# A mixture of 32 experts on one core: SwiGLU once an expert, weighted one-hots on ScalarE, float32 matmuls in larger groups, first-layer weights by 2 MB

## The chip, the cores and the metric

The kernel is one program on one core of a Trainium2 chip. The metric is the device time of one execution in microseconds; lower is better. The engines named below are TensorE (PE, its weight loads PEld), VectorE (DVE), ScalarE (ACT), GpSimd (POOL) and SyncE (SP), which here only issues transfers.

## The reference

Two model blocks over 256 tokens of width 1024, in float32. The first has two layers of feed-forward network, mixer and feed-forward network; the second has a mixer and then the part that the change touches, a mixture of 32 experts of which each token takes 4:

```python
logits = tokens @ w_router + b_router
top_logits, top_idx = lax.top_k(logits, 4); top_w = softmax(top_logits)
# for each expert e, for the tokens that chose it:
hid = tokens[rows] @ w_exp_in[e] + b_exp_in[e]            # 1024 -> 2048
x_glu = minimum(hid[..., ::2], 7);  x_lin = clip(hid[..., 1::2], -7, 7)
out = (x_glu * sigmoid(1.702 * x_glu) * (x_lin + 1)) @ w_exp_out[e] + b_exp_out[e]   # 1024 -> 1024
y[rows] += out * top_w
```

After it come a gate, the addition to x and a last rmsnorm.

## The kernel before, in words

All weights are float32 in HBM, 713 MB with the rest, and pass through the core once, in the order of use, as a **stream** (class `Stream`) of chunks of 128 rows x 2048 columns, 1 MB. SyncE issues a chunk's load (L272) as soon as its **place** is free. A chunk is split by halves (`convert`): ScalarE writes `wh`, the half rounded to the matmul's short float32 format (L284), and VectorE writes `wl`, the remainder `raw - wh` (L285). TensorE multiplies with both. There are five pairs `wh`, `wl`, so the conversions run up to five halves ahead of TensorE. `get()` hands out the next pair; each call is one **step**, and `later(PRE or POST, n, f)` puts off a piece of work by n steps, ahead of or behind the conversions of that step. All queues follow the order in which the program issues, which this code lays down by hand.

In the dense part, up to some 1600 us, the stream has three places of 1 MB (pool `raw`). At the end of the second mixer four buffers of 1 MB that are no longer needed (`p2`, tags r0 to r3) become places too, and the two of `xt` once each; in the experts' part the seven places take the chunks in turn.

The experts' part is the function `moe`. Each expert has 64 slots, and one-hot matrices gather the tokens into them (`Group`, four experts at a time; `gather`). A loop runs q = 0 to 132; q = 4 e + j calls `hidden(e, j)`, which multiplies the slots with a quarter of the first-layer weights (two chunks `exp_in`, four steps), and from q = 5 on `outputs`, a quarter of the second layer of the expert before (one chunk `exp_out`, two steps). `folded` brings a quarter of the hidden units, copied out of PSUM as `hs`, into the transposed form by float32 matmuls `pf`, and after every second quarter runs the SwiGLU on half an expert's units: add the bias (L1555), clip (L1556, L1557), multiply (L1558), sigmoid on ScalarE (L1562), multiply (L1563), and split into two parts `act` (L1564 on ScalarE, L1565 on VectorE). When both quarters of an output half are summed, `combine` adds it to the tokens' sums `y` by float32 matmuls (L1523) with weighted, transposed one-hots `ohw`. These come from `wdup`, one-hot times weight, made on GpSimd (L1493) and turned by TensorE (L1500). A float32 matmul stands as two records in the trace.

```python
        for q in range(4 * NE + 5):
            e, j = divmod(q, 4)
...
                hidden(e, j)
            if q >= 5:
                outputs(*divmod(OUT_ORDER[q - 5], 4))
```

## Time and profile before

| | us |
|---|---|
| median of three runs (lowest, highest) | 2688.63 (2688.14, 2689.32) |
| the profiled execution, its span | 2688.0 |
| TensorE, VectorE, ScalarE busy in it | 2605.0, 2080.7, 1723.2 |
| the experts' stretch shown below, 1700 to 2600 us: VectorE busy | 890.54 of 900 |

The profile records one execution; busy times are sums over its instructions, and a share over the whole span mixes the dense part, to some 1600 us, with the experts' part after it. Tables by stretches keep them apart. A matmul's end is modelled, so that a busy TensorE is not TensorE at its peak.

### The profile page before, as it was taken

To read this page: it belongs to the slowest core of one execution; us is meant where nothing else is said; L and a number is where in the kernel's file an instruction comes from. 1 tells how busy PE (TensorE), PEld (TensorE's weight loads), DVE (VectorE), ACT (ScalarE), POOL (GpSimd) and SP (SyncE) were. 2 spreads that over 40 slices of the span, in tenths; PEclk is the share of its full clock that TensorE was granted. 3 is DMA by queue.
4 is the path that set the end of the run, shared out by engine and by line. 5 is a ranking of instruction groups with operands and counts; after the bars stand their busy time and mean duration, and the time that the engine had idled before them with its cause. 6 is when DMAs were issued, how large, how long until landed. Compare 5 with 4: busy or idle time off the path is not lost.

```text
span 2688.0 us, 34842 instructions
## 1 busy us (share of the span) xinstructions
PE 2605.0 (97%) x12700; PEld 2092.6 (78%) x12700; DVE 2080.7 (77%) x2717; ACT 1723.2 (64%) x2290; POOL 182.6 (7%) x255
## 2 busy tenths in 40 slices
PE   8999999999999999999999998999999999999996
PEld 6889888887787978778798886777777777777775
DVE  5656766666666676655656679999999999999997
ACT  5444554444444454544555538989898989888886
POOL 1000000001101000000000102000000000000000
PEclk9999999999999999999999999999999999999999
DMA  7655445655566444565444566999999999999995
GB/s 282 220 216 207 153 149 192 221 218 211 213 225 245 149 153 172 193 226 180 158 149 151 175 246 251 381 399 389 381 393 388 386 388 391 388 393 389 390 395 203
DMA packets 106227, 712.89 MB, mean 265 GB/s; under 512 B 13380, under 2 KB 14052, under 8 KB 25409
## 3 DMA queue, kind: packets, MB, share of 16 engines
q1 hardware_dynamic: 92976, 667.03, 65.9%
q0 software_dynamic: 12928, 43.05, 4.3%
q8 instruction: 101, 1.65, 0.2%
q14 instruction: 78, 0.63, 0.1%
q10 hardware_dynamic: 144, 0.52, 0.0%
HBM read 709.40 MB, written 3.77 MB: 265 GB/s over the span
## 4 chain that ended last, share of the span: by engine, by line
PE 84%; DVE 9%; issue 3%; ACT 3%; DMA 0%; POOL 0%; DVEq 0%; SPq 0%; ACTq 0%; POOLq 0%
PE hid L1536 7%; PE hid L1537 6%; DVE wl L285 6%; PE po L1580 3%; PE pf L1549 3%; PE g L347 3%; PE u L347 3%; PE g L348 3%; PE u L349 3%; PE g L349 3%; PE u L348 3%; PE d L347 3%; PE d L349 3%; PE d L348 3%; PE y L1523 3%
## 5 line engine op out<-in xcount | busy, mean ns | idle before, releaser
L285 DVE TENSOR_TENSOR wl<-raw,wh 128x1024 fp32r<-128x1024 f32 (+2 forms) x1274 | 1504.7, 1218 | 424.7 <-ACT wh L284 414.9
L284 ACT ACTIVATE wh<-raw 128x1024 fp32r<-128x1024 f32 (+2 forms) x1274 | 1294.3, 1050 | 527.7 <-PE d L349 126.5
L1536 PE MATMUL hid<-wh,xgt 128*128 128x512 f32 x1024 | 441.0, 431 | 0.2 <-ACT hs L1539 0.2
L1537 PE MATMUL hid<-wl,xgt 128*128 128x512 f32 x1024 | 404.8, 395 | 0.0
L1580 PE MATMUL po<-wl,act 128*128 128x512 f32 x512 | 208.6, 407 | 32.9 <-DVE wl L285 32.9
L1536 PEld LDWEIGHTS hid<-wh,xgt 128*128 128x128 f32 x1024 | 193.3, 189 | 54.3 <-issue 16.1
L1537 PEld LDWEIGHTS hid<-wl,xgt 128*128 128x128 f32 x1024 | 193.3, 189 | 53.3 <-issue 14.3
L1579 PE MATMUL po<-wh,act 128*128 128x512 f32 x512 | 204.0, 398 | 2.8 <-ACT osb L1584 2.8
L1580 PEld LDWEIGHTS po<-wl,act 128*128 128x128 f32 x512 | 96.1, 188 | 78.5 <-DVE wl L285 57.6
L347 PE MATMUL g<-wh,xth 128*128 128x512 f32 (+1 forms) x384 | 147.0, 383 | 0.0
L347 PE MATMUL u<-wh,xth 128*128 128x512 f32 (+1 forms) x384 | 146.0, 380 | 0.0
L348 PE MATMUL g<-wl,xth 128*128 128x512 f32 (+1 forms) x384 | 144.8, 377 | 0.0
L349 PE MATMUL g<-wh,xtl 128*128 128x512 f32 (+1 forms) x384 | 144.5, 376 | 0.0
L349 PE MATMUL u<-wh,xtl 128*128 128x512 f32 (+1 forms) x384 | 144.4, 376 | 0.0
L348 PE MATMUL u<-wl,xth 128*128 128x512 f32 (+1 forms) x384 | 144.1, 375 | 0.0
L347 PE MATMUL d<-wh,hth 128*128 128x512 f32 x352 | 139.8, 397 | 0.0
L349 PE MATMUL d<-wh,htl 128*128 128x512 f32 x352 | 138.8, 394 | 0.0
L348 PE MATMUL d<-wl,hth 128*128 128x512 f32 x352 | 138.8, 394 | 0.0
L1549 PEld LDWEIGHTS pf<-fold,hs 128*128 128x128 f32 x1024 | 130.8, 192 | 8.8 <-issue 1.3
L1549 PE MATMUL pf<-fold,hs 128*128 128x64 f32 x1024 | 129.1, 269 | 1.4 <-DVE v L1555 0.9
L1523 PE MATMUL y<-osb,ohw 128*128 128x512 f32 x256 | 123.0, 603 | 2.1 <-ACT osb L1584 2.1
L1493 POOL TENSOR_TENSOR wdup<-oh,wgt 128x128 f32<-128x128 f32 x64 | 72.5, 1162 | 741.4 <-PE wts L1500 510.0
(488 smaller groups left out, 4441.6 us busy)
## 6 DMA issues: line engine op xcount, KB each, us to landing
raw<-d_exp_in SPq DMA_DIRECT2D x256, 1024.0 KB, 7.3
raw<-d_dense SPq DMA_DIRECT2D x245, 1024.0 KB, 4.8
raw<-d_exp_out SPq DMA_DIRECT2D x128, 1024.0 KB, 7.5
ada_w<-d_ada POOLq DMA_DIRECT2D x96, 256.0 KB, 4.6
bias<-tables POOLq DMA_DIRECT2D x2, 1920.0 KB, 12.7
bg<-d_b_gate POOLq DMA_DIRECT2D x12, 256.0 KB, 4.2
raw<-d_dense SPq DMA_DIRECT2D x4, 768.0 KB, 4.5
raw<-d_dense SPq DMA_DIRECT2D x5, 512.0 KB, 3.6
```

What stands on the lines that cost most here:

```text
L284: A.activation(hi[:, :w], r[:, h * w:h * w + w], AF.Copy)
L285: V.tensor_tensor(lo[:, :w], r[:, h * w:h * w + w], hi[:, :w], OP.subtract)
L347: T.matmul(ps, lhsT=xh, rhs=wh, start=start, stop=False)
L348: T.matmul(ps, lhsT=xh, rhs=wl, start=False, stop=False)
L349: T.matmul(ps, lhsT=xl, rhs=wh, start=False, stop=stop_)
L1493: G.tensor_tensor(d[:, :, c], oh, wg, OP.mult)
L1523: T.matmul(y[t][n], lhsT=grp[e // 4].w[:, e % 4, t], rhs=osb[e, n], start=e == 0, stop=e == NE - 1)
L1536: T.matmul(ph, lhsT=lhs, rhs=wh[:, 512 * i:512 * i + 512], start=k == 0, stop=False)
L1537: T.matmul(ph, lhsT=lhs, rhs=wl[:, 512 * i:512 * i + 512], start=False, stop=k == 7)
L1549: T.matmul(pf[:, 4 * (c // 2) + 2 * (j % 2) + c % 2], lhsT=hs[:, 128 * c:128 * c + 128], rhs=fold, start=True, stop=True)
L1579: T.matmul(po, lhsT=lhs, rhs=wh[:, 512 * i:512 * i + 512], start=k == 0, stop=False)
L1580: T.matmul(po, lhsT=lhs, rhs=wl[:, 512 * i:512 * i + 512], start=False, stop=k == 7)
```

## The change

It has four parts, all in the experts' part; the dense part's instructions keep their order.

1. **SwiGLU once an expert.** `folded` is called once for two quarters, does their `pf` matmuls in one group, and adds the bias into half of `v`, which now holds a whole expert. `activate` does the rest over 512 columns after the second half; the last expert still goes by halves.
2. **Weighted one-hots on ScalarE**: eight copies with a scale per group of four experts, in place of GpSimd's eight multiplications.
3. **`combine` once an expert**: the four matmuls `y` of both output halves follow one another.
4. **First-layer weights by 2 MB.** Two chunks `exp_in` become one of 128 x 4096. Places are kept by size: r0 to r3 and the dense places 0 and 1 become three places of 2 MB, `xt` one of 2 MB used once; the chunks `exp_out` keep the third dense place, and from q = 14 a second one, `hx`, in the space of the pool `bp`, which is given up at q = 14 in place of 26 (`bias_part` and `bias_sum` move to q = 8, 10 and 12 for it). The two rows that `gated_sum` and `final` need are loaded at q = 128 into a place. The two parts of a converted half lie in one tile `w`.

```diff
-        a["w_exp_in_2"][0].reshape(NE, 2, 4, 128, 4, 256, 2).transpose(0, 4, 1, 3, 2, 6, 5)
-    ).reshape(NE, 4, 2, 128, 2048)
+        a["w_exp_in_2"][0].reshape(NE, 2, 4, 128, 4, 256, 2).transpose(0, 4, 3, 1, 2, 6, 5)
+    ).reshape(NE, 4, 128, 4096)
...
+            self.todo = {w: [i for i, (_, n) in enumerate(chunks) if (n > 2048) == (w > 2048)] for w in (2048, 4096)}
+            self.own = raw.tile([128, 2048 * RAW], FT, name="raw")
+            self.free, self.held = {2048: list(range(RAW)), 4096: []}, []
...
+                ready = [w for w in (2048, 4096) if self.free[w] and self.todo[w]]
+                if not ready:
+                    break
+                w = min(ready, key=lambda w: self.todo[w][0])
+                i = self.todo[w].pop(0)
...
+        def done(self, i):
+            del self.R[i]
+            p = self.T.pop(i)
+            if p not in self.once:
+                w = 4096 if self.ch[i][1] > 2048 else 2048
+                if w == 2048 and p in (0, 1) and self.todo[2048] and self.todo[2048][0] >= DENSE:
+                    self.held.append(p)
+                    if len(self.held) == 2:
+                        self.free[4096].append(0)
+                else:
+                    self.free[w].append(p)
+                self.load()
...
+                    both = self.part("w")
+                    hi, lo = both[:, :1024], both[:, 1024:]
...
-            dense += [(I["exp_in"][q // 4, q % 4, h], 2048) for h in range(2)]
+            dense.append((I["exp_in"][q // 4, q % 4], 4096))
...
-        st.more(p2, ("r2", "r3", "r0", "r1"))
+        st.more(p2, ("r23", "r01"), 4096)
...
-        st.more(xtp[0], ("xth", "xtl"), once=True)
+        st.more(xtp[0], ("xt",), 4096, once=True)
...
-                    oh = self.oh[:, t].rearrange("p (a b) -> p a b", a=4)[:, e:e + 2]
-                    wg = rep(wgt[:, t, 4 * self.g + e:4 * self.g + e + 2], SL, 2)
-                    for c in range(2):
-                        G.tensor_tensor(d[:, :, c], oh, wg, OP.mult)
+                    oh = self.oh[:, t].bitcast(FT)
+                    for i in range(2):
+                        n = 4 * self.g + e + i
+                        A.activation(d[:, i], rep(oh[:, SL * (e + i):SL * (e + i + 1)], 2, 1), AF.Copy,
+                                     scale=wgt[:, t, n:n + 1])
...
-                later(POST, 6, turn)
+                later(POST, 4, turn)
...
-            later(POST, 3 if e < NE - 1 or j < 3 else 2, lambda: folded(e, j, hs))
-        pfs = {}
-        def folded(e, j, hs):
-            if j % 2 == 0:
-                pfs[0] = pfp.tile([128, 8, SL], FT, name="pf")
-            pf = pfs[0]
-            for c in range(4):
-                T.matmul(pf[:, 4 * (c // 2) + 2 * (j % 2) + c % 2], lhsT=hs[:, 128 * c:128 * c + 128], rhs=fold,
-                         start=True, stop=True)
-            if j % 2 == 0:
-                return
-            hf = j // 2
-            v = w2.tile([128, 8, SL], FT, name="v")
-            V.tensor_tensor(v, pf, rep(ebias[:, e, 8 * hf:8 * hf + 8], SL, 2), OP.add)
-            V.tensor_scalar(v[:, 0:4], v[:, 0:4], 7.0, None, op0=OP.min)
-            V.tensor_scalar(v[:, 4:8], v[:, 4:8], 7.0, -7.0, op0=OP.min, op1=OP.max)
-            V.scalar_tensor_tensor(v[:, 4:8], v[:, 4:8], 1.0, v[:, 0:4], op0=OP.add, op1=OP.mult)
-            sg = w2.tile([128, 4, SL], FT, name="sg")
-            hi, lo = (act[e][:, 4 * hf:4 * hf + 4, i] for i in range(2))
-            d = 3 if e < NE - 1 or j < 3 else 2
-            later(PRE, d, lambda: A.activation(sg, v[:, 0:4], AF.Sigmoid, scale=1.702))
-            later(POST, d, lambda: V.tensor_tensor(v[:, 4:8], v[:, 4:8], sg, OP.mult))
-            later(PRE, 2 * d, lambda: A.activation(hi, v[:, 4:8], AF.Copy))
-            later(POST, 2 * d, lambda: V.tensor_tensor(lo, v[:, 4:8], hi, OP.subtract))
+            hss[j % 2] = hs
+            if j % 2:
+                later(POST, 3 if e < NE - 1 or j < 3 else 2, lambda e=e, j=j, h=dict(hss): folded(e, j // 2, h))
+        hss, vs = {}, {}
+        def folded(e, hf, hss):
+            pf = pfp.tile([128, 2, 4, SL], FT, name="pf")
+            for j in range(2):
+                for c in range(4):
+                    T.matmul(pf[:, c // 2, 2 * j + c % 2], lhsT=hss[j][:, 128 * c:128 * c + 128], rhs=fold,
+                             start=True, stop=True)
+            if hf == 0:
+                vs[0] = w1.tile([128, 2, 8, SL], FT, name="v")
+            v = vs[0]
+            b = ebias[:, e, 8 * hf:8 * hf + 8].rearrange("p (a b) -> p a b", a=2)
+            V.tensor_tensor(v[:, :, 4 * hf:4 * hf + 4], pf, rep(b, SL, 3), OP.add)
+            if e == NE - 1:
+                activate(e, 4 * hf, 4 * hf + 4, 3 - hf)
+            elif hf:
+                activate(e, 0, 8, 3 if e else 2)
+        def activate(e, lo_, hi_, d):
+            glu, lin = vs[0][:, 0, lo_:hi_], vs[0][:, 1, lo_:hi_]
+            V.tensor_scalar(glu, glu, 7.0, None, op0=OP.min)
+            V.tensor_scalar(lin, lin, 7.0, -7.0, op0=OP.min, op1=OP.max)
+            V.scalar_tensor_tensor(lin, lin, 1.0, glu, op0=OP.add, op1=OP.mult)
+            sg = w1.tile([128, hi_ - lo_, SL], FT, name="sg", tag="sg")
+            hi, lo = (act[e][:, lo_:hi_, i] for i in range(2))
+            later(PRE, d, lambda: A.activation(sg, glu, AF.Sigmoid, scale=1.702))
+            later(POST, d, lambda: V.tensor_tensor(lin, lin, sg, OP.mult))
+            later(PRE, 2 * d, lambda: A.activation(hi, lin, AF.Copy))
+            later(POST, 2 * d, lambda: V.tensor_tensor(lo, lin, hi, OP.subtract))
...
-                    later(POST, 3, lambda: [combine(e, n, t) for t in range(2)])
+                    if n:
+                        later(POST, 3, lambda: [combine(e, m, t) for m in range(2) for t in range(2)])
...
-            if q == 17:
+            if q == 8:
                 later(POST, 1, bias_part)
-            if q in (20, 22):
-                later(POST, 1, lambda: bias_sum(q // 2 - 10))
+            if q in (10, 12):
+                later(POST, 1, lambda: bias_sum(q // 2 - 5))
             if q == 12:
                 count = nc.values_load(router.most[:, 0:1], min_val=0, max_val=S,
                                        skip_runtime_bounds_check_because="a count of at most S tokens")
-            if q == 26:
+            if q == 14:
                 leave("bp")
-                fp = enter("fin", 1, side="right")
-                for src in (bcast_row(mods, D, 3 * D), bcast_row(I["final_norm"], D)):
-                    fin.append(fp.tile([128, D], FT, name=f"fin{len(fin)}"))
-                    G.dma_start(fin[-1], src)
+                st.more(enter("hx", 1, side="right"), ("hx",), 2048)
+            if q == 4 * NE:
+                fin.extend(st.rows((bcast_row(mods, D, 3 * D), bcast_row(I["final_norm"], D))))
```

VectorE's queue in the middle of the experts' part, one expert's half before (`wl<-raw,wh` are the subtractions that split the weights; a row ends in its count):

```order
L1555 TENSOR_TENSOR v<-pf,ebias 128x512
L1556 TENSOR_SCALAR v<-v 128x256
L1557 TENSOR_SCALAR v<-v 128x256
L1558 SCALAR_TENSOR_TENSOR v<-v 128x256
L285 TENSOR_TENSOR wl<-raw,wh 128x1024 x3
L1563 TENSOR_TENSOR v<-v,sg 128x256
L285 TENSOR_TENSOR wl<-raw,wh 128x1024 x3
L1565 TENSOR_TENSOR act<-v,act 128x4x64
L285 TENSOR_TENSOR wl<-raw,wh 128x1024 x6
```

and an expert's cycle in the changed kernel (`w<-raw,w` is the same subtraction):

```order
L336 TENSOR_TENSOR w<-raw,w 128x1024 x6
L1647 TENSOR_TENSOR v<-pf,ebias 128x2x256
L336 TENSOR_TENSOR w<-raw,w 128x1024 x12
L1647 TENSOR_TENSOR v<-pf,ebias 128x2x256
L1655 TENSOR_SCALAR v<-v 128x512
L1656 TENSOR_SCALAR v<-v 128x512
L1657 SCALAR_TENSOR_TENSOR v<-v 128x512
L336 TENSOR_TENSOR w<-raw,w 128x1024 x3
L1661 TENSOR_TENSOR v<-v,sg 128x512
L336 TENSOR_TENSOR w<-raw,w 128x1024 x3
L1663 TENSOR_TENSOR act<-v,act 128x8x64
```

Before, the six SwiGLU rows stand once for 12 subtractions; now the addition stands once for 12, and the five others once for 24, twice as wide.

SyncE's queue at q = 9 to 11 before (each `raw_` with a number is a tile of its own, in the next of the seven places):

```order
L272 DMA raw_13671<-d_exp_in 128x2048
L272 DMA raw_13699<-d_exp_out 128x2048
L272 DMA raw_13729<-d_exp_in 128x2048
L272 DMA raw_13752<-d_exp_in 128x2048
L272 DMA raw_13787<-d_exp_out 128x2048
L272 DMA raw_13806<-d_exp_in 128x2048
L272 DMA raw_13827<-d_exp_in 128x2048
L272 DMA raw_13861<-d_exp_out 128x2048
```

and about q = 11 to 15 in the changed kernel (`raw_80` is the tile of the dense places: its form 128x4096 is the 2 MB of places 0 and 1, its form 128x2048 the third place; `raw_13458` is `hx`; `TENSOR_LOAD` reads a count of tokens into a register):

```order
L295 DMA raw_13237<-d_exp_in 128x4096
L295 DMA raw_80<-d_exp_out 128x2048
L295 DMA raw_80<-d_exp_in 128x4096
L1718 TENSOR_LOAD most_11946
L295 DMA raw_80<-d_exp_out 128x2048
L295 DMA raw_13373<-d_exp_in 128x4096
L295 DMA raw_80<-d_exp_out 128x2048
L295 DMA raw_13442<-d_exp_in 128x4096
L295 DMA raw_13458<-d_exp_out 128x2048
L295 DMA raw_80<-d_exp_out 128x2048
```

Before, each `exp_out` has a place other than the one ahead of it; now every `exp_out` up to `hx` goes into the one place of the `exp_out` ahead of it, and behind an `exp_in` of 2 MB.

## Rows read from the trace of the kernel before

**Rows 1.** The page's totals: engine, busy us, share of the span, instructions.
```profile
PE 2605.0 (97%) x12700; PEld 2092.6 (78%) x12700; DVE 2080.7 (77%) x2717; ACT 1723.2 (64%) x2290; POOL 182.6 (7%) x255
```

**Rows 2.** Table by stretches: length, busy us of each engine, PEclk, DMA share, GB/s.
```profile
1590.00:1600.00 10.00, 10.00 (x49) 8.17 (x48) 8.15 (x8) 4.16 (x5) 0.00 (x0) 1.00 1.01 424
1630.00:1640.00 10.00, 9.43 (x50) 7.62 (x49) 7.58 (x10) 9.97 (x15) 4.20 (x5) 1.00 0.76 256
1640.00:2660.00 1020.00, 979.22 (x4559) 751.75 (x4559) 1009.73 (x1149) 908.83 (x1141) 69.96 (x63) 1.00 0.97 383
1700.00:2600.00 900.00, 869.18 (x4042) 667.66 (x4040) 890.54 (x1013) 802.61 (x1009) 58.69 (x54) 1.00 0.99 389
```

**Rows 3.** Groups from 1700 to 2600 us: count, busy us, mean ns, idle before.
```profile
L285 DVE TENSOR_TENSOR wl<-raw,wh 128x1024 fp32r<-128x1024 f32 x666 | 774.7, 1220 | 5.6 <-ACT wh L284 1.3
L284 ACT ACTIVATE wh<-raw 128x1024 fp32r<-128x1024 f32 x665 | 664.2, 1051 | 7.0 <-PE hid L1536 6.3
L1523 PE MATMUL y<-osb,ohw 128*128 128x512 f32 x220 | 105.8, 603 | 2.1 <-ACT osb L1584 2.1
...
L1558 DVE SCALAR_TENSOR_TENSOR v<-v 128x256 f32<-128x256 f32 x56 | 24.0, 428 | 1.9
L1562 ACT ACTIVATE sg<-v 128x256 f32<-128x256 f32 x56 | 23.4, 418 | 47.2 <-DVE v L1556 47.2
L1556 DVE TENSOR_SCALAR v<-v 128x256 f32<-128x256 f32 x56 | 18.8, 336 | 1.9
L1557 DVE TENSOR_SCALAR v<-v 128x256 f32<-128x256 f32 x56 | 18.6, 333 | 0.0
```

**Rows 4.** Waits from 1700 to 2600 us: total us, times, longest.
```profile
PEld po L1580 <- DVE wl L285: 51.2, 54, 2.3
...
ACT wh L284 <- PE hid L1536: 6.3, 4, 2.1
DVE wl L285 <- ACT wh L284: 1.3, 3, 0.5
```

**Rows 5.** Waits of SyncE's queue in the same stretch.
```profile
SPq L272 <- DVE wl L285: 647.9, 271, 4.5
```

**Rows 6.** Timeline of VectorE: start us, length us, instruction.
```profile
2004.29 0.42 DVE L1565 TENSOR_TENSOR act<-v,act 128x256 fp32r<-128x256 f32 x1
2004.62 6.90 DVE L285 TENSOR_TENSOR wl<-raw,wh 128x1024 fp32r<-128x1024 f32 x6
2011.44 0.69 DVE L1555 TENSOR_TENSOR v<-pf,ebias 128x512 f32<-128x512 f32 x1
2012.16 0.29 DVE L1556 TENSOR_SCALAR v<-v 128x256 f32<-128x256 f32 x1
2012.37 0.28 DVE L1557 TENSOR_SCALAR v<-v 128x256 f32<-128x256 f32 x1
2012.69 0.43 DVE L1558 SCALAR_TENSOR_TENSOR v<-v 128x256 f32<-128x256 f32 x1
2013.03 3.49 DVE L285 TENSOR_TENSOR wl<-raw,wh 128x1024 fp32r<-128x1024 f32 x3
```

**Rows 7.** Groups of VectorE before 1600 us, two with 512 columns.
```profile
L455 DVE SCALAR_TENSOR_TENSOR ada_acc<-ada_w,ada_c,ada_acc 128x512 f32<-128x512 f32 x84 | 62.7, 746 | 0.0
L453 DVE TENSOR_SCALAR ada_acc<-ada_w,ada_c 128x512 f32<-128x512 f32 x12 | 5.8, 481 | 0.0
```

**Rows 8.** Single lines from 1700 to 2600 us: duration ns min/median/max.
```profile
L1556 DVE TENSOR_SCALAR v<-v x56: 293/294/495, 1701.9 to 2594.5; 128x256 f32<-128x256 f32 x56
...
L1557 DVE TENSOR_SCALAR v<-v x56: 284/286/506, 1702.1 to 2594.7; 128x256 f32<-128x256 f32 x56
...
L1493 POOL TENSOR_TENSOR wdup<-oh,wgt x52: 393/442/4676, 1728.8 to 2514.7; 128x128 f32<-128x128 f32 x52
```

**Rows 9.** SyncE's line L272: landing from 1700 to 2600 and 1640 to 1700.
```profile
DMA to landing us min/median/max: 5.8/7.4/9.1
...
DMA to landing us min/median/max: 4.7/5.0/6.6
```

More of the change, by code (lines that the diff above doesn't have):

```diff
@@ L292, in more @@
[L292 to L298 removed]
+                self.R[i] = r
+            if not self.todo[4096]:
+                self.free[2048] += self.free[4096]
+                self.free[4096] = []
+        def done(self, i):
[10 more added lines that the diff above has]
+                self.load()
```

184 lines of the change are left out of this document (114 added, 70 removed).

## Prediction, written before the run

> **What bounds the kernel now.** I began with the line of engine totals: TensorE is busy for 2605 of 2688 us [rows 1], which invites the thought that only TensorE matters. The table by stretches corrects it for the experts' part, and nothing outside that part changes its order on any engine. From 1700 to 2600 us VectorE is busy 890.54 of 900 us, and from 1640 to 2660 us 1009.73 of 1020 us; TensorE has 30.8 us idle in the 900, ScalarE 97 [rows 2]. The 666 `wl` subtractions of the 900 us, 24 an expert, say that 27.75 experts passed: 900 / 27.75 = 32.43 us for one. The list of waits names the order of command: TensorE waits for VectorE's `wl` (51.2 us, 54 times), while VectorE waits for ScalarE 1.3 us in all, and ScalarE for TensorE's release of a pair 6.3 us [rows 4]. Nobody waits for a transfer; SyncE, which issues them, waits 647.9 us for VectorE to free a place [rows 5]. So although the transfers keep the DMA share at 0.99 and 389 GB/s [rows 2], in this stretch VectorE sets the pace.
>
> VectorE's 32.43 us can be added up from the timeline. Six `wl` in a row take 2011.44 - 2004.62 = 6.82 us, 1.137 each from start to start (a duration of 1.22 overlaps its neighbour by some 0.08). One half's SwiGLU takes, start to start, 0.72 (`v`), 0.21 and 0.32 (two clips), 0.34 (product), and 0.33 each for the product with the sigmoid and for `lo`: 2.25 [rows 6]. 24 x 1.137 + 2 x 2.25 = 31.8; one-hots and collisions with GpSimd make up the rest.
>
> **The change, part by part.** Durations are from the one profiled execution, span 2688.0 us; the median of the runs shown is 2688.63, so I add 0.6 at the end.
>
> *SwiGLU once an expert.* VectorE keeps two additions `v` of 512 columns and has one of each other operation over 512 where it had two over 256: 7 instructions for 12. What does an instruction cost beyond its columns? `lo` with 256 columns starts 0.33 us before its successor, a `wl` with 1024 takes 1.137 [rows 6]: 0.807 / 768 = 1.05 ns a column, and 0.33 - 0.27 = 0.06 us fixed. Five instructions fewer save 5 x 0.06 = 0.3. The additions save more: `v` takes 0.72 because the clip waits for it, where 512 columns by that line take 0.60, and the second clip takes 0.32 against 0.21 before a dependent one. Each of these two waits now occurs once: 0.12 + 0.11. Together 0.53, the lower bound. For the upper one I take durations of the dense part at 512 columns, 481 for a clip and 746 for the three-operand form [rows 7]: 2 x 294 - 481, 2 x 286 - 481 [rows 8] and 2 x 428 - 746 [rows 3] save 0.11, 0.09 and 0.11; with two more like the last, 0.53, and the two waits on top, 0.76. I take 0.6 an expert, since the starts are what VectorE pays.
>
> [...]
>
> *Weighted one-hots on ScalarE.* GpSimd's 52 `wdup` disappear from the stretch. Beside them VectorE's clips take 495 and 506 ns where the median is 294 and 286, and they themselves reach 4676 ns against 442 [rows 8]: the two engines hold each other up. Means of 336 and 333 [rows 3] over medians of 294 and 286, 56 times each, are 5.0 us; with a little on the `wl`, 5.6 us, 0.2 an expert. ScalarE has 97 us to spare in 900 and takes 8 copies per four experts, each no more than the 418 ns of `sg` with 256 columns [rows 3]: hidden. Only at 1630 to 1640, where ScalarE is busy for 9.97 of 10 us and VectorE for 7.58 [rows 2], do the first 8 lie on the path: up to 3.3 us, I take 2.
>
> So VectorE gains 0.8 us an expert. The last expert keeps its halves: 31 x 0.8 = **-25**, bounds 31 x 0.53 = -16 and 31 x 0.96 = -30.
>
> *One place for the second-layer chunks.* Before, every chunk of 1 MB takes the next of seven places. Now chunk `exp_out` has one place of its own until q = 14, when `hx` joins. The nine chunks 1 to 9 (q = 6 to 14, all beyond 1640 us) can only be issued when VectorE has finished the second half of the one before. The place's cycle: landing L, then ScalarE's `wh` 1.05, VectorE's two `wl` 1.22 and 1.14 [rows 3, 6], and 0.2 that I allow for the hand-overs: L + 3.6 us, against a q of 32.43 / 4 less 0.2 = 7.9. Landing takes 7.4 us in the median and 5.8 to 9.1 in the steady stretch, 4.7 to 6.6 from 1640 to 1700 [rows 9]. I work L out: a 2 MB transfer, 4.9 us long at the 424 GB/s of the fill [rows 2], was issued two `wl` (2.3 us) and the wait s itself ahead, so that the chunk's own 4.7 us start late by 4.9 - 2.3 - s: L = 7.3 - s. With s = L + 3.6 - 7.9 that gives s = 1.5 and L = 5.8. Nine of these: **+14**, bounds 9 x 0.4 = 4 (L = 4.7) and 9 x 3.1 = 28 (L = 7.4). ScalarE's `wh` will wait for a transfer here; behind it in its queue stand the other `wh` and the copies `hs` and `osb`, so that TensorE's `pf` and `y` come late with it; on VectorE the SwiGLU stands behind the `wl`. On SyncE the next 2 MB stands behind the 1 MB's issue, but three to four places ahead of need. After q = 14 a chunk is issued more than one q ahead, over 12 us against 9.1: nothing.
>
> *Larger float32 groups.* The work of `pf` and `y` is the same; their groups are twice as long. A `y` record lasts 603 ns [rows 3], so that four more in a row delay the next weights by up to 2.4 us, and VectorE, at most five pairs (5.7 us) ahead, may run into TensorE. Today that costs 6.3 us in 900 [rows 4]; doubled or tripled it adds 6 to 12, at best nothing. I take **+3**. `lo` over all 512 columns lands one `wl` before its first use; TensorE waits there some 0.6 us more, which its 30.8 us idle pays.
>
> *2 MB transfers.* 128 issues fewer on SyncE, which idles; DMA bytes are the same: nothing, if landing stays in front of need (three to four places of 2 MB, 16 us or more). Bias product earlier, final rows from SyncE at the end, tiles merged: nothing, TensorE waits there and the DMA rate falls off at the end.
>
> Sum: -25 + 14 + 2 + 3 = -6; 2688.0 - 6 + 0.6 = **2682.6 us**.
>
> **The rivals.**
> (a) *The transfers become the bound*, the one on the other side. An expert is 12 chunks of 1 MiB, 12.58 MB; at 389 GB/s that is 32.3 us, today's period. With 0.8 us less the chip must deliver 12.58 / 31.63 = 398 GB/s; from that figure it decides. For it: share 0.99 [rows 2], landing 7.4 against 5.0 [rows 9]. Against it: 424 GB/s in the fill [rows 2], and no wait for a transfer. Then the 25 us are not had: 2688 + 14 + 2 + 0.6 = 2705. [...]
> (b) *The wait on the single place is nearly free*: L near 4.7 because the 2 MB transfers have long passed. Then +4: 2672. For it: 4.7 to 5.0 us before 1700 [rows 9].
> (c) *The wait is long*, L at the steady 7.4: -25 + 28 + 5 = +8, 2697. For it: the same DMA share in the steady stretch; against it: while VectorE waits, no new 2 MB is issued.
> (d) *TensorE takes over.* Its idle time, 30.8 / 27.75 = 1.11 us an expert [rows 2], exceeds the 0.8 by little. If the longer groups leave half of it unusable, the gain is 0.55 x 31 = 17: -17 + 14 + 2 = -1, 2687.6. For it: the present waits in both directions [rows 4].
>
> **How the numbers follow.** 0.2% is 5.4 us, about what a measurement of this kernel can tell from no change: 2683.3 to 2694.0 is within. Chances: the forecast 0.42 (its own range 2676 to 2687, so 0.30 faster, 0.12 within), (b) 0.19, faster; (d) 0.17, mostly within; (c) 0.12, slower in three quarters; (a) 0.10, slower. Faster 0.50, within 0.29, slower 0.21. The extreme bounds are 2688.6 - 30 + 4 = 2663 and, with (c) or (a), 2688.6 - 16 + 28 + 2 + 12 = 2715; (a) alone ends at 2705. Leaving out what is beyond 2702 of these two, about one in seven, and little below, the range is 2665 to 2702.
>
> **What the profile after would show.** VectorE's share still near 0.99 from 1740 on and the period, 24 `wl`, at 31.6 us; clips without the 495 ns cases; no `wdup` on GpSimd; the DMA rate near 398 GB/s. Between 1650 and 1740 ScalarE's `wh` waiting for a transfer nine times by 1 to 3 us. ScalarE's `wh` waiting for TensorE by more than 6.3 us per 900 would show the cost of the groups. I am wrong if ScalarE waits for transfers past 1740 (a), if the nine waits are missing or above 3 us (b, c), or if TensorE has hardly any idle time left while VectorE has (d).

## The result, and the profile after

The changed kernel takes 2712.24 us (median of four, 2710.74 to 2712.27) beside 2688.39: a ratio of 1.0084, interval 1.0071 to 1.0097. It is 0.84% slower, where the forecast was 2682.6, faster by 0.2%, and the range ended at 2702. The profiled execution has a span of 2710.5 us.

The two traces agree to 2 us up to 1640 us. To see where the time goes afterwards, an instruction that both kernels run twice an expert serves as a milestone: VectorE's bias addition `v` (L1555 before, L1647 after). The 8th and the last of the 64, on the timeline of VectorE (start us, length us), before:

```profile
1749.66 0.68 DVE L1555 TENSOR_TENSOR v<-pf,ebias 128x512 f32<-128x512 f32 x1
...
2656.20 0.68 DVE L1555 TENSOR_TENSOR v<-pf,ebias 128x512 f32<-128x512 f32 x1
```

and after:

```profile
1773.52 0.68 DVE L1647 TENSOR_TENSOR v<-pf,ebias 128x512 f32<-128x512 f32 x1
...
2677.03 0.68 DVE L1647 TENSOR_TENSOR v<-pf,ebias 128x512 f32<-128x512 f32 x1
```

At the 8th the changed kernel is 23.9 us late, at the last 20.8. So the loss is made in the first four experts, and the 28 experts after them win back 3 us, 0.1 an expert, where the prediction had 0.8. These are two questions, and the table by stretches (length, busy us of PE, PEld, DVE, ACT, POOL, PEclk, DMA share, GB/s) shows both. The start before:

```profile
1640.00:1740.00 100.00, 94.57 (x461) 73.47 (x460) 99.12 (x115) 89.81 (x116) 17.05 (x13) 1.00 0.91 352
```

and both stretches after:

```profile
1640.00:1740.00 100.00, 86.56 (x371) 66.43 (x371) 76.36 (x78) 74.24 (x97) 0.00 (x0) 0.90 0.76 284
1740.00:2600.00 860.00, 827.45 (x3843) 635.82 (x3842) 832.13 (x832) 763.98 (x963) 0.00 (x0) 0.99 0.98 387
```

From 1640 to 1740 VectorE, with 99.12 us nearly full before, works 76.36 us of 100. From 1740 to 2600 it works 832.13 of 860; before, it idled 9.5 us in 900 [rows 2]. TensorE idles 32.6 us of 860, 30.1 before.

The waits of the first stretch (total us, times, longest) after:

```profile
DVE w L336 <- ACT w L335: 22.4, 15, 4.1
ACT w L335 <- DMA raw<-d_exp_out: 14.9, 6, 4.9
ACT w L335 <- PE hid L1618: 6.9, 5, 4.1
```

one turn of it on ScalarE's timeline (an idle time ahead of an instruction, and what ended it, stands in brackets),

```profile
1684.37 3.90 ACT L335 ACTIVATE w<-raw 128x1024 fp32r<-128x1024 f32 x4 [3.09 <-DMA raw<-d_exp_out]
...
1692.74 1.06 ACT L335 ACTIVATE w<-raw 128x1024 fp32r<-128x1024 f32 x1 [1.62 <-DMA raw<-d_exp_out]
...
1703.27 3.90 ACT L335 ACTIVATE w<-raw 128x1024 fp32r<-128x1024 f32 x4 [0.45 <-DMA raw<-d_exp_out]
```

and on SyncE's, which issues:

```profile
1687.84 0.33 SPq L295 DMA_DIRECT2D raw<-d_exp_out  x1
1692.38 0.33 SPq L295 DMA_DIRECT2D raw<-d_exp_in  x1
1698.34 0.33 SPq L295 DMA_DIRECT2D raw<-d_exp_out  x1
```

ScalarE waits 3.09 us for a second-layer chunk at 1684. Chunks are issued at 1687.84 and again at 1698.34, 10.5 us apart: that is one cycle of the one place. From 1667.17 to 1749.66 us there are eight such cycles, 10.3 us each in the mean, where the prediction had 9.4. Waits for a second-layer chunk number nine, as forecast: the six of this stretch and three more that end by 1765, 20.8 us together.

The waits of the steady stretch after, which answer to [rows 4]:

```profile
PEld po L1618 <- DVE w L336: 48.9, 42, 2.3
ACT w L335 <- PE hid L1618: 44.0, 52, 2.0
...
DVE w L336 <- ACT w L335: 24.8, 45, 3.0
...
ACT w L335 <- DMA raw<-d_exp_out: 6.5, 4, 2.6
```

TensorE waits for VectorE as before, at the output matmuls; but ScalarE now waits 44.0 us for TensorE to release a pair, against 6.3, and VectorE waits 24.8 us for ScalarE, against 1.3 [rows 4]. TensorE and VectorE now wait for each other in turn. Transfers are waited for 6.5 us; 5.9 of these are the last three of the nine waits, and 6.1 us of VectorE's waits lie there too.

VectorE's work falls, by a little less than forecast. Of its groups in this stretch after (mean ns ahead of the last bar),

```profile
L336 DVE TENSOR_TENSOR w<-raw,w 128x1024 fp32r<-128x1024 f32 x635 | 734.7, 1218 | 26.1 <-ACT w L335 24.8
...
L1661 DVE TENSOR_TENSOR v<-v,sg 128x512 f32<-128x512 f32 x27 | 18.4, 683 | 0.0
...
L1655 DVE TENSOR_SCALAR v<-v 128x512 f32<-128x512 f32 x26 | 11.1, 427 | 0.9
```

the clip with 512 columns lasts 427 ns with no GpSimd beside it, where two lasted 336 each [rows 3]. 635 conversions are 26.46 experts, so VectorE works 832.13 / 26.46 = 31.45 us an expert. From 1740 to 2600 us the kernel before has 850.88 us with 637 conversions, 32.06 an expert (the row with 850.88 is shown with the experiments). The saving of 0.6 us is there; it stands as idle time.

This stretch still holds the end of the start's waits. To compare periods, 25 whole experts are better, from the 10th to the 60th `v`: 811.67 us before (1782.11 to 2593.78), 32.47 an expert, of which VectorE is busy for 32.12; 808.50 us after (1805.50 to 2614.00), 32.34, with VectorE busy for 31.47. Of 0.65 us saved, 0.13 became time. Periods below are taken in this way.

### The profile page after: what moved, and what is told of

Its sections match the earlier page's. It is cut to its first block, busy times and chain, and to the rows that moved or that the text cites. A ratio compares the mean times of both kernels' runs of the same rounds, so it can differ in the third digit from the quotient of the medians.

```text
span 2710.5 us, 33808 instructions
## 1 busy us (share of the span) xinstructions
PE 2619.3 (97%) x12700; PEld 2101.8 (78%) x12700; DVE 2060.1 (76%) x2562; ACT 1724.0 (64%) x2292; POOL 108.7 (4%) x189
## 4 chain that ended last, share of the span: by engine, by line
PE 71%; DVE 16%; ACT 7%; issue 3%; DMA 2%; POOL 0%; ACTq 0%; SPq 0%; POOLq 0%; DVEq 0%
DVE w L336 12%; ACT w L335 5%; PE hid L1618 3%; PE u L411 3%; PE g L411 3%; PE g L412 3%; PE g L413 3%; PE u L413 3%; PE u L412 3%; PE d L411 3%; PE d L413 3%; PE d L412 3%; PE hid L1617 3%; PE z L411 3%; PE z L412 2%
## 5 line engine op out<-in xcount | busy, mean ns | idle before, releaser
L336 DVE TENSOR_TENSOR w<-raw,w 128x1024 fp32r<-128x1024 f32 (+2 forms) x1274 | 1499.1, 1216 | 471.6 <-ACT w L335 466.3
L335 ACT ACTIVATE w<-raw 128x1024 fp32r<-128x1024 f32 (+2 forms) x1274 | 1293.0, 1051 | 601.9 <-PE d L413 126.6
L1617 PE MATMUL hid<-w,xgt 128*128 128x512 f32 x1024 | 429.2, 419 | 3.4 <-ACT ohw L1578 3.1
L1618 PE MATMUL hid<-w,xgt 128*128 128x512 f32 x1024 | 413.7, 404 | 1.0 <-DVE w L336 1.0
L1618 PE MATMUL po<-w,act 128*128 128x512 f32 x512 | 209.2, 409 | 39.6 <-DVE w L336 39.6
L1618 PEld LDWEIGHTS hid<-w,xgt 128*128 128x128 f32 x1024 | 195.7, 191 | 63.5 <-DVE w L336 20.4
L1617 PEld LDWEIGHTS hid<-w,xgt 128*128 128x128 f32 x1024 | 195.9, 191 | 52.1 <-issue 8.7
L1617 PE MATMUL po<-w,act 128*128 128x512 f32 x512 | 205.2, 401 | 7.0 <-ACT osb L1677 3.0
L1618 PEld LDWEIGHTS po<-w,act 128*128 128x128 f32 x512 | 97.3, 190 | 82.2 <-DVE w L336 59.1
L411 PE MATMUL g<-w,xt 128*128 128x512 f32 (+1 forms) x384 | 147.4, 384 | 0.0
L411 PE MATMUL u<-w,xt 128*128 128x512 f32 (+1 forms) x384 | 146.1, 380 | 0.0
L412 PE MATMUL g<-w,xt 128*128 128x512 f32 (+1 forms) x384 | 145.1, 378 | 0.5 <-DVE w L336 0.5
L413 PE MATMUL g<-w,xt 128*128 128x512 f32 (+1 forms) x384 | 144.6, 377 | 0.0
L413 PE MATMUL u<-w,xt 128*128 128x512 f32 (+1 forms) x384 | 144.3, 376 | 0.0
L412 PE MATMUL u<-w,xt 128*128 128x512 f32 (+1 forms) x384 | 144.1, 375 | 0.0
L411 PE MATMUL d<-w,hth 128*128 128x512 f32 x352 | 139.8, 397 | 0.0
L413 PE MATMUL d<-w,htl 128*128 128x512 f32 x352 | 138.8, 394 | 0.0
L412 PE MATMUL d<-w,hth 128*128 128x512 f32 x352 | 138.8, 394 | 0.0
L1617 PEld LDWEIGHTS po<-w,act 128*128 128x128 f32 x512 | 97.2, 190 | 29.3 <-ACT osb L1677 3.5
```

Of the source, the lines that this page charges most:

```text
L335: A.activation(hi[:, :w], r, AF.Copy)
L336: V.tensor_tensor(lo[:, :w], r, hi[:, :w], OP.subtract)
L411: T.matmul(ps, lhsT=xh, rhs=wh, start=start, stop=False)
L412: T.matmul(ps, lhsT=xh, rhs=wl, start=False, stop=False)
L413: T.matmul(ps, lhsT=xl, rhs=wh, start=False, stop=stop_)
L1617: T.matmul(ps, lhsT=x, rhs=wh[:, sl], start=start, stop=False)
```

## The experiments

Three theories stood at the start. *The single place*: the 24 us at the start are the nine waits for a second-layer chunk. *The pairs*: in the steady stretch TensorE's work is nearly as long as VectorE's, and with five pairs between them the longer groups make each wait for the other, so that VectorE's saving does not shorten the period. *The transfers*, rival (a): 390 GB/s is all that the chip delivers here, and the period is theirs.

**Three places until q = 14** (`e1_out3`).

```diff
-                if w == 2048 and p in (0, 1) and self.todo[2048] and self.todo[2048][0] >= DENSE:
+                if w == 2048 and p in (0, 1) and self.todo[2048] and i >= DENSE and self.merge:
...
                 st.more(enter("hx", 1, side="right"), ("hx",), 2048)
+                st.merge = True
```

> The changed kernel, but the second-layer chunks keep all three dense places until q = 14 (the 2 MB place made of two of them comes only then). Theory of the single place: the nine waits of ScalarE for a second-layer transfer go, and with them 20 to 26 us, 2686 to 2692 us; the steady period stays. Rival (the start is lost to the 2 MB transfers, the earlier bias product or ScalarE's copies): 2708 us or more.

2696.56 us, ratio 1.0025 (1.0015 to 1.0034): 15.7 us less than the changed kernel. The table by stretches:

```profile
1640.00:1740.00 100.00, 91.52 (x426) 70.68 (x425) 87.74 (x89) 85.55 (x116) 0.00 (x0) 0.97 0.84 322
1740.00:2600.00 860.00, 829.28 (x3863) 640.61 (x3861) 836.43 (x837) 767.26 (x961) 0.00 (x0) 0.99 0.98 390
```

VectorE is back to 87.74 us in the first stretch, and no second-layer chunk is waited for there. The mechanism holds, at 15.7 us, less than the 20 to 26 that I expected; the 8th `v` comes 17.8 us earlier than in the changed kernel, at 1755.76. Some 6 us of the start stay; the run with the one-hots alone accounts for about half of them. The steady period hardly changes, 32.40 us against 32.34.

**y in twos** (`e2_y2`), on the changed kernel.

```diff
-                    if n:
-                        later(POST, 3, lambda: [combine(e, m, t) for m in range(2) for t in range(2)])
+                    later(POST, 3, lambda: [combine(e, n, t) for t in range(2)])
```

> The changed kernel with the matmuls y again in two groups of two an expert. Theory of the pairs (VectorE and TensorE stop each other in turn, since five pairs do not cover the longer groups): ScalarE's 55 us of waits for TensorE fall to half or less and 5 to 15 us are gained, 2697 to 2707. Rival (the transfers' rate of 390 GB/s sets the steady period): within 3 us of 2712.

2700.22 us, ratio 1.0035 (1.0021 to 1.0049): 12 us gained, within the range that the theory of the pairs gave; the period falls to 32.06 us. But the wait that I named, ScalarE's for TensorE, was to fall to half, and did not. The waits from 1740 to 2600 us:

```profile
ACT w L335 <- PE hid L1618: 62.5, 85, 1.1
PEld y L1599 <- ACT osb L1677: 34.4, 28, 1.8
...
PE y L1599 <- ACT osb L1677: 22.1, 26, 1.4
...
PEld po L1618 <- DVE w L336: 12.8, 16, 1.3
```

It grows to 62.5 us, and a new one appears: TensorE's `y` waits for `osb`, ScalarE's copy of an output half out of PSUM. What falls is TensorE's wait for VectorE at the output matmuls, from 48.9 to 12.8 us.

**Four pairs** (`e3_hl4`) and **half the second-layer bytes** (`e4_halfout`), both on the changed kernel.

```diff
+        st.hl.pop(0)                                   # e3_hl4, at the start of moe
...
+                if i >= DENSE and n == 2048 and self.merge:   # e4_halfout, in load
+                    n = 1024
+                    self.short.add(i)
...
+                if i in self.short:                    # in convert
+                    h = 0
```

> The changed kernel with four pairs in place of five in the experts' part. Theory of the pairs: VectorE and TensorE wait more for each other, 1 us or more an expert, 2740 us or more. Rival (transfers): the waits move, the period does not, within 6 us of 2712.

> The changed kernel, but from q = 14 on only the first half of each second-layer chunk is loaded and it is converted and multiplied twice, so that a sixth of the transferred bytes is left out and no other work. Rival (transfers set the period): the period falls from 32.5 to 31.6 us or below, some 25 us, 2690 or less. Theory of the pairs: within 5 us of 2712.

2758.34 us (1.0250; 1.0233 to 1.0267) and 2712.57 us (1.0087; 1.0070 to 1.0104). A pair less costs 46 us; a sixth of the bytes less brings nothing, with the DMA share at 0.87 and 324 GB/s:

```profile
1740.00:2600.00 860.00, 827.11 (x3846) 635.97 (x3845) 831.91 (x831) 763.67 (x960) 0.00 (x0) 1.00 0.87 324
```

The period is 32.34 us with all the bytes and without the sixth. The transfers do not set it. Rival (a) is out.

**Each part alone, on the kernel before.** The edits are those of the change: the SwiGLU (`e5_swiglu`), the one-hots (`e6_wdup`), `combine` once an expert (`e7_comb`), and the three together without the 2 MB part (`e8_123`).

> The kernel before with the SwiGLU part alone (with its longer groups of pf); transfers of 1 MB, one-hots on GpSimd and y in twos as before. VectorE's saving of 0.6 us an expert, if nothing stood against it: 2670. Theory of the pairs: the burst of VectorE (0.7 + 0.35 + 0.45 + 0.6 us without a subtraction) and the 16 records of pf make the two engines wait for each other, so that half or less arrives: 2678 to 2688.

> The kernel before with the weighted one-hots on ScalarE alone. VectorE without collisions gains 0.2 us an expert, 6 us, less 2 us at the start: 2682 to 2688. Rival: the copies on ScalarE delay the conversions and the gain is lost, 2689 or more.

> The kernel before with the four matmuls y of an expert in one group alone; no work is added. Theory of the pairs: ScalarE's waits for TensorE (6.3 us in the stretch of 900) grow several times, 5 to 15 us slower, 2693 to 2704. If the group's length is harmless: 2687 to 2691.

> The kernel before with the first three parts, and the transfers and places as before (seven places of 1 MB in turn): the 2 MB part undone. Theory of the single place for the start and of the pairs for the rest: no wait for a transfer, the start as before, a gain of 0.1 to 0.2 us an expert: 2684 to 2690. If the 2 MB transfers had hurt the steady stretch: 2675 or less.

| run | us | ratio, interval |
|---|---|---|
| SwiGLU alone | 2682.40 | 0.9975 (0.9963 to 0.9986) |
| one-hots alone | 2692.03 | 1.0011 (1.0001 to 1.0021) |
| y in fours alone | 2742.84 | 1.0199 (1.0182 to 1.0216) |
| the three, 1 MB transfers | 2696.43 | 1.0030 (1.0020 to 1.0039) |

The SwiGLU part gains 7 us of the 18 that its 0.6 an expert would be. The one-hots, which should have gained 6 less 2 at the start, cost some 3: their rival came true. `combine`, which adds no work, costs 54 us by itself, where I had expected 5 to 15, and yet the three together cost only 7, outside the 2684 to 2690 that I expected of them: the costs do not add up, which is what one expects of waits and not of work. The three with 1 MB transfers end where the changed kernel with three places does (2696.43 and 2696.56, periods 32.38 and 32.40), so that the 2 MB transfers as such are worth nothing, as forecast. The waits of the run with the one-hots alone, from 1638 to 1665 us,

```profile
PEld hid L1537 <- ACT ohw L1503: 4.4, 1, 4.4
```

and from 1740 to 2600:

```profile
DVE wl L285 <- ACT wh L284: 6.7, 10, 0.8
```

At the start TensorE waits 4.4 us at one stroke for `ohw`: the copy stands on ScalarE behind the new `wdup` copies, and until it is done holds one of the two tiles of the PSUM pool `psH`, from which `hid` takes its own too. (The edit also lets TensorE turn the one-hots two steps earlier, `later(POST, 4, turn)`; the two were not separated.) Later VectorE waits 6.7 us for ScalarE, where it waited 1.3 [rows 4]. In the kernel before, from 1700 to 2600 us, every clip of 0.48 us or more, 25 of 112, lies beside a `wdup` on GpSimd; here VectorE's work falls from 32.12 to 31.94 us an expert, and this relief comes back as idle time.

The waits of the `combine` run from 1740 to 2600 us,

```profile
PEld po L1580 <- DVE wl L285: 88.5, 105, 2.4
...
ACT wh L284 <- PE hid L1536: 55.4, 27, 3.2
...
DVE wl L285 <- ACT wh L284: 37.2, 50, 2.3
```

and its group on TensorE's timeline:

```profile
2032.27 3.62 PE L1523 MATMUL y<-osb,ohw 128*128 128x512 f32 x8
```

The group takes 3.62 us, in which VectorE would make 3.62 / 1.137 = 3.2 pairs. VectorE loses 37.2 us to ScalarE, which loses 55.4 to TensorE; TensorE then loses 88.5 to VectorE, against 51.2 [rows 4]. The period is 34.10 us.

A part of this may be TensorE's clock. Ahead of the group above TensorE waits 1.53 us for `wl`; soon after, the clock granted in the 3.5 us up to 2032 is 0.55, and most `hid` records last 0.63 us, where most lasted 0.39 to 0.40 before the wait (length, TensorE's busy us, PEclk, DMA share, GB/s):

```profile
2025.00:2028.50 3.50, 1.97 (x12) 1.00 0.97 403
2028.50:2032.00 3.50, 3.50 (x13) 0.55 1.05 363
```

Taken by stretches of 5 us, the clock that is missing, (1 - PEclk) x 5 us, adds up to 13.6 us over this run's 25 experts, to 1.7 on the kernel before, to 3.5 on the changed one, and to nothing with y in twos (e2). So at most 12 of the 41 us that `combine` costs in these 25 experts, and 3.5 of the 7 by which the changed kernel stands above its version with y in twos there, are slower matmuls. No run separates them from the waits.

For the SwiGLU alone the timelines show where the pairs are held up. VectorE,

```profile
2208.34 0.68 DVE L1573 TENSOR_TENSOR v<-v,sg 128x512 f32<-128x512 f32 x1
```

ScalarE,

```profile
2209.06 0.63 ACT L1574 ACTIVATE act<-v 128x512 fp32r<-128x512 f32 x1 [0.66 <-DVE v L1573]
2209.60 0.58 ACT L1594 ACTIVATE osb<-po 128x512 f32<-128x512 f32 x1
```

and TensorE:

```profile
2210.23 1.98 PE L1524 MATMUL y<-osb,ohw 128*128 128x512 f32 x4 [0.51 <-ACT osb L1594]
```

ScalarE's `act` waits 0.66 us for VectorE's product, which stands there behind three subtractions; `osb` stands behind `act` in ScalarE's queue; and TensorE's `y` waits 0.51 us for `osb`, with all the matmuls that would release pairs behind it. Before, `osb` stood behind an `act` too, but a half's operations take 0.42 us each [rows 3, 6], and these 0.68 and 0.63: half a microsecond later, `osb` has lost its lead. (This last step is a reading of single turns; the runs with y five steps behind, below, test it.)

**Is VectorE really the bound of the kernel before?** Two runs on it, without its product with the sigmoid (`e9_nomult`) and without half the `y` matmuls (`e10_halfy`).

```diff
-            later(POST, d, lambda: V.tensor_tensor(v[:, 4:8], v[:, 4:8], sg, OP.mult))    # e9_nomult
...
+            if t == 0 or e in (0, NE - 1):                                                # e10_halfy
                 T.matmul(y[t][n], lhsT=grp[e // 4].w[:, e % 4, t], rhs=osb[e, n], start=e == 0, stop=e == NE - 1)
```

> The kernel before without VectorE's product with the sigmoid (left out, 64 instructions of 0.33 us from start to start, 21 us; nothing else changes). If VectorE alone sets the pace of the steady stretch, as the prediction has it, nearly all of it comes back: 2667 to 2672. If TensorE is nearly as slow and the two stop each other, a third to two thirds: 2675 to 2683.

> The kernel before without the matmuls y of half the tokens for experts 1 to 30 (left out; 1.7 us of TensorE's time an expert). If VectorE alone sets the pace, nothing: 2686 to 2691. If TensorE and VectorE stop each other, 10 us or more: 2679 or less.

2668.18 us (0.9918; 0.9902 to 0.9935) and 2688.69 us (0.9998; 0.9988 to 1.0008). My expectation of a partial return was wrong: all of VectorE's 21 us come back, and leaving out half the `y` matmuls brings nothing, though TensorE is busy for 1.3 us an expert less, where I had written 1.7 (from 1740 to 2600 us 829.92 with 637 conversions before, 794.28 with 636 in e10). The reading of the profile before was right. The rows of before and of the run without the product, 1740 to 2600 us:

```profile
1740.00:2600.00 860.00, 829.92 (x3855) 637.34 (x3854) 850.88 (x967) 766.94 (x963) 52.91 (x50) 1.00 0.99 390
```

```profile
1740.00:2600.00 860.00, 841.11 (x3933) 652.69 (x3932) 852.30 (x934) 780.67 (x982) 51.47 (x50) 1.00 1.00 398
```

Without the product the DMA engines move 398 GB/s, the figure from which rival (a) decided. So a saving on VectorE can arrive in full, where it takes an instruction out and leaves the places of all the others in the order alone. One thing besides VectorE's work goes with the product: ScalarE's `act` no longer waits for it, which it did for 36.5 us from 1740 to 2600 before; this run does not tell the two apart.

**Both mendings** (`e11_out3_y2`, the edits of e1 and e2), **and a sixth pair** (`e12_six`, which makes these edits besides).

```diff
-        actp = enter("act", 3)
+        actp = enter("act", 2)
-                self.oh = w2.tile([128, 2, 256], FR, name="oh") if g else router.oh
+                self.oh = w1.tile([128, 2, 256], FR, name="oh") if g else router.oh
-            sg = w1.tile([128, hi_ - lo_, SL], FT, name="sg", tag="sg")
+            sg = glu
...
                 st.more(enter("hx", 1, side="right"), ("hx",), 2048)
+                st.hl.append((enter("hl6", 1, side="right"), "c5"))
```

> The changed kernel with both mendings, three places for second-layer chunks until q = 14 and y in twos. If the two costs add up: 2696.6 - 12 = 2684.6, 2681 to 2688. If they share one cause, 2690 or more.

> The same with a sixth pair from q = 14 on (its room comes from two act tiles in place of three, one one-hot tile in place of two, and the sigmoid written over its input). Theory of the pairs: the waits in both directions shrink and the period goes to VectorE's own 31.6 us, 15 to 25 us below the kernel without the sixth pair, 2660 to 2670. Rival (the order of the work, not the depth, makes the waits): within 5 us of that kernel.

2687.19 us (0.9992; 0.9983 to 1.0002) and 2699.05 us (1.0035; 1.0023 to 1.0048). Mended in both places, the change is worth nothing that can be measured. The sixth pair, with what was given up to make room for it, costs 12 us where I expected a gain of 15 to 25: this edit, as I had put it, does not bring the saving out. TensorE's waits for `osb` are longest in this run:

```profile
PEld y L1599 <- ACT osb L1677: 45.1, 28, 3.0
PE y L1599 <- ACT osb L1677: 32.9, 28, 2.6
```

The work that `later` puts off is queued behind the conversions of its step. My reading was that a deeper line of conversions puts VectorE's product, and with it `act` and `osb`, later against TensorE's steps. It is not shown: the room came from other places, and one of them makes a wait of its own, as the next runs show.

**y five steps behind its output half**, on the SwiGLU part alone (`e13_sw_y5`), on the kernel with both mendings (`e14_mend_y5`), and on that with the sixth pair (`e15_six_y5`).

```diff
-                    later(POST, 3, lambda: [combine(e, n, t) for t in range(2)])
+                    later(POST, 5, lambda: [combine(e, n, t) for t in range(2)])
```

> The kernel with the SwiGLU part alone (2682.4 us), and the matmuls y five steps behind their output half in place of three. Theory of the queue behind act: on ScalarE the copy osb stands behind act, which waits for VectorE's product, so that TensorE's y waits for osb (30 and 18 us) and gives up the pairs late; two steps more take the wait away, and 5 to 12 us of the missing gain come: 2670 to 2677. Rival (the longer groups of pf and the depth of five pairs): within 3 us of 2682.

> The changed kernel with three places until q = 14, y in twos (2687.2 us), and y five steps behind. Theory of the queue behind act: TensorE's waits for osb (33 and 22 us) go, 2674 to 2681. Rival (depth): within 3 us of 2687.

> The same with a sixth pair from q = 14 (2699.1 us with y three steps behind). Theory of the queue behind act: a deeper line of conversions puts VectorE's product, and with it act and osb, later against TensorE's steps, which is why the sixth pair cost 12 us; with y five steps behind it costs nothing, within 5 us of the kernel with five pairs or below. Rival (the room for the sixth pair, two act tiles, costs it): 8 us or more above that kernel.

2677.95 us (0.9956; 0.9940 to 0.9973), 2683.28 us (0.9975; 0.9965 to 0.9984) and 2691.82 us (1.0009; 0.9999 to 1.0019). Moving y is worth some 4 us in the first two, just short of the 5 to 12 and 6 to 13 that I expected; the intervals of each pair of runs overlap, but the periods fall too, from 32.16 to 31.96 and from 32.05 to 31.93. The same move on the kernel before was not run; there TensorE's `y` waits for `osb` 2.1 us in 900 [rows 3], so that little could come of it. Of the 0.58 us an expert that VectorE saves in the SwiGLU run, 0.51 now arrive. Both engines are nearly full there, TensorE with 843.12 of 860 us and VectorE with 849.33:

```profile
1740.00:2600.00 860.00, 843.12 (x3920) 646.31 (x3919) 849.33 (x849) 763.51 (x924) 64.73 (x50) 1.00 1.00 396
```

The sixth pair still costs 8.5 us, where I had written that it would cost nothing, and that 8 or more would speak for the room it takes. The waits show two that are new in this run:

```profile
PEld po L1617 <- DVE act L1663: 32.0, 26, 1.6
ACT v L1660 <- DVE v L1657: 29.1, 27, 2.2
```

With y out of the way, TensorE waits for `lo`, VectorE's last operation on `act`. And the sigmoid, which for room is now written over its input, must wait until VectorE's product (L1657) has read that input, 29.1 us in 860; with a tile of its own, in e14, it waited for the first clip alone:

```profile
ACT sg L1660 <- DVE v L1655: 2.1, 6, 0.4
```

Yet none of these waits lengthens the period: it is 31.97 us, against 31.93 in e14. In the profiled executions 1.5 of the sixth pair's 6.3 us arise ahead of the 10th `v`, 0.9 in the 25 experts and 3.9 behind them, where the last expert ends. (With y three steps behind, e12 against e11, it is 3.1, 5.7 and 4.1 of 12.9.) So the depth does no harm to the steady stretch here; which part of the edit costs the rest was not separated.

**A sixth pair on the kernel with y in fours alone** (`e16_comb_six`), from q = 26 on; the last rows go to a dense place.

```diff
-                fp = enter("fin", 1, side="right")
+                st.hl.append(enter("hl6", 1, side="right"))
```

> The kernel before with the four y in one group (2742.8 us) and a sixth pair from q = 26 on. Theory of the pairs for this group: 3.6 us of TensorE without a release are 3.2 conversions, which with what VectorE is already ahead exceeds five; with six most of the 54 us go, 2715 or less. Rival (the group delays something else): 2733 or more.

2714.68 us (1.0092; 1.0076 to 1.0109), 28 of the 54 us back, just inside the 2715 that I had set, with the pair present in four fifths of the experts' part. Here depth accounts for half of the cost; the clock that is missing, counted as above, falls with it, from 13.6 to 6.9 us. What is left is in part a wait of TensorE's `pf` for `hs`, 52.3 us in 860, of the same kind as the one for `lo`.

**The changed kernel without half the y matmuls** (`e17_after_halfy`), the edit of `e10_halfy`, and **SwiGLU and one-hots with y five steps behind** (`e18_12_y5`).

> The changed kernel without the matmuls y of half the tokens for experts 1 to 30 (left out, 1.7 us of TensorE's time an expert). On the kernel before the same brought nothing. If TensorE's time and the length of its group now keep VectorE's saving from showing: the period falls from 32.5 to 31.6 us, 18 to 26 us, 2686 to 2694. If VectorE, the transfers or ScalarE's queue hold the steady stretch: 2707 or more.

> The kernel before with the SwiGLU part, y five steps behind (2678.0 us) and the one-hots on ScalarE, none of the other parts. If the one-hots' relief of VectorE shows once y no longer waits: 2672 to 2675. If the copies on ScalarE take as much as the collisions, as in the run with the one-hots alone: 2678 to 2682.

2693.55 us (1.0011; 1.0001 to 1.0021) and 2679.35 us (0.9962; 0.9948 to 0.9976). What brought nothing on the kernel before brings 19 us on the changed one:

```profile
1740.00:2600.00 860.00, 820.70 (x3815) 619.89 (x3815) 846.34 (x850) 779.26 (x983) 0.00 (x0) 0.99 0.98 396
```

The period is 31.64 us, against 32.34. The saving of VectorE shows. But the run with all of the y matmuls, in twos and five steps behind (e14), comes to 31.93: the length and the place of TensorE's groups account for more than half of what hid the saving, and the amount of its work for the rest at most. The one-hots on ScalarE gain nothing in the best version either: 2679.35 against 2677.95.

The lowest time of a version that leaves nothing out is that of the SwiGLU part alone with y five steps behind its output half, 2677.95 us, 0.44% below the kernel before; e18 cannot be told apart from it.

## Why the prediction was wrong, point by point

**What bounds the kernel before** was read rightly: e9 and e10 show that VectorE sets the pace. **The 2 MB transfers** as such cost nothing (e1 against e8), and **rival (a)** is out (e4, and 398 GB/s in e9).

**The wait on the single place** was right in its mechanism and close in its size: +14 forecast, 15.7 measured by its removal. The nine waits came, of 2.3 us in the mean where the sum had 1.5. The landing was about as worked out, 5.8 us: 5.5 in the median for the chunks of 1 MB issued from 1640 to 1740 us,

```profile
raw<-d_exp_in SPq DMA_DIRECT2D x9, 2048.0 KB, 7.7
raw<-d_exp_out SPq DMA_DIRECT2D x8, 1024.0 KB, 5.5
```

and 6.0 in the mean of the first eight waits, from a chunk's issue to the end of the wait for it. What the cycle of 10.3 us has beyond 9.4 lies mostly behind the landing, where 3.5 to 5.6 us pass until the next issue, 4.3 in the mean, in place of 3.6. **The one-hots at the start**, +2, are about 3 (e6), but by another way: not the 3.3 us of the copies on ScalarE, but TensorE's wait for `ohw`.

**The step that failed is "So VectorE gains 0.8 us an expert ... -25".** It took VectorE's saving for time, with the waits of the three engines left as they were but for +3. The start made +24 us where 14 + 2 were forecast; the experts after it made -3 where -25 + 3 were. VectorE's work did fall, by 32.12 - 31.47 = 0.65 us an expert, of which the SwiGLU alone gives 0.5 (e5) and the one-hots alone 0.2 (e6). But most of it did not become time. For the 25 experts from the 10th to the 60th `v`, in us an expert:

| kernel | 10th and 60th `v`, start us | period | VectorE busy | the rest |
|---|---|---|---|---|
| before | 1782.11, 2593.78 | 32.47 | 32.12 | 0.35 |
| before, no product (e9) | 1778.90, 2573.88 | 31.80 | 31.50 | 0.30 |
| SwiGLU alone (e5) | 1782.75, 2586.78 | 32.16 | 31.62 | 0.54 |
| the same, y five steps behind (e13) | 1781.23, 2580.15 | 31.96 | 31.54 | 0.42 |
| one-hots alone (e6) | 1785.05, 2597.14 | 32.48 | 31.94 | 0.54 |
| after | 1805.50, 2614.00 | 32.34 | 31.47 | 0.87 |
| after, y in twos and three places (e11) | 1791.77, 2593.11 | 32.05 | 31.47 | 0.59 |
| the same, y five steps behind (e14) | 1791.12, 2589.41 | 31.93 | 31.37 | 0.56 |
| after, half the y left out (e17) | 1803.66, 2594.74 | 31.64 | 31.31 | 0.33 |

The change brought VectorE to 31.47, where e9 has 31.50 and a period of 31.80. The change's own order put 0.5 us an expert of new waits on top: 0.3 are the four y in one group (after to e11; the three places leave the period as it is, e1), and 0.2 stay, which go only where half the y matmuls are left out (e17). Moving y by two steps (e14) takes another 0.12 off the period, though mostly off VectorE's busy time, which no run explains. TensorE has little room to make up for such waits: its own work is 31.4 us an expert before and 31.2 after, as the profile models it. That is rival (d) in its second half, the longer groups that leave TensorE's idle time unusable, to which I gave 0.17. Its sign did not come, however: TensorE still has 32.6 us of idle time in 860, and VectorE 27.9. I had put 17 us there for what would be left of the saving; 3 arrived. And the range was drawn too short: the bounds of (c) and (a) went to 2715, which would have held the 2712, and it ends at 2702.

**"Larger float32 groups, +3"** was mis-sized: 12 in the changed kernel (e2), 54 on the kernel before (e7), where four `y` matmuls hold back the pairs for 3.6 us, nearly twice as long as before. I had scaled today's wait of 6.3 us by two or three, and the cost of the longer group has no relation to the 6.3. Five pairs are 5.7 us of conversions, so a group of 3.6 us should fit where VectorE is fully ahead; that it is not ahead so far at that point is argued, not shown. e16 shows the depth of the pairs for half of the 54, and slower matmuls may be a part, as said there.

**"The one-hots' relief"** is real on VectorE, but came as idle time: in e6 VectorE's waits for ScalarE grow by as much, and the period stays (32.48 against 32.47). I had counted ScalarE's spare time in the mean, and not its queue.

What stays open: why `combine` alone costs so much more on the kernel before than with the SwiGLU once an expert beside it, of which the phase between VectorE's burst and TensorE's group is a likely cause but only an argued one, with TensorE's clock as another part of it (13.6 us against 3.4 in e8); and the 0.2 us an expert above. Of the start little stays open. The 8th `v` is later than before by 23.9 us in the changed kernel, 6.1 in e1, 4.2 with the first three parts (e8), 3.0 with the one-hots alone and 1.2 with the SwiGLU alone: so the three parts explain 4.2, and some 2 belong to the 2 MB part besides the single place. In e1 ScalarE waits once, 2.7 us, for a first 2 MB chunk, but no run isolates this.

## What to carry to other kernels

In this kernel a saving on the engine that sets the pace arrived in full where only an instruction was taken out (21 of 21 us), and not where the rewrite that brought it also lengthened groups and moved work: price the saving and the new order apart, each by a run of its own. A longer group was not neutral, though it was shorter than what the full set of buffers holds (3.6 us against 5.7): it is safer to measure it alone than to scale a small wait of today. Look in each engine's queue for what now stands behind a wait (here `osb` behind `act`; moving one matmul group by two steps was worth some 4 us). And when buffers are divided among kinds, work out the cycle of the kind that is left with one place.

## What the runs showed that I had not expected

A sixth pair of buffers, with the room that was made for it, left the kernel slower by 12 and by 8.5 us, though on the kernel with y in fours, with other room, it won 28. The edit that bought space by writing over an input added a wait of its own (29.1 us of ScalarE's time above). And the granted clock of TensorE falls at the start of the experts' part. TensorE's busy time, PEclk, DMA share and GB/s in the changed kernel, by 5 us:

```profile
1640.00:1645.00 5.00, 5.00 (x26) 1.00 0.91 315
1645.00:1650.00 5.00, 1.86 (x8) 0.86 0.25 108
1650.00:1655.00 5.00, 5.00 (x19) 0.50 0.94 334
1655.00:1660.00 5.00, 4.94 (x19) 0.61 0.20 85
```

Behind the wait for `ohw`, in which TensorE works 1.86 us of 5, the clock granted is 0.50 for the next 5 us, and the `hid` records last 0.63 us there, where most lasted 0.39 to 0.40 ahead of the wait. In the stretch of 1640 to 1740 us the mean of the clock is 0.90, and 0.97 with three places, where TensorE is busy for 91.52 us in place of 86.56; what the waits cost includes the slower clock behind them.
